# Attention results and turns of the fourth unit kind in pairs at every second token step, with separate tiles for the conditioning rows

## The chip, the cores and the metric

The kernel runs on one core of a Trainium2 chip. The metric is the device time of one execution in microseconds, the median of several. Before the change it is 1508.83 us (three runs, 1507.0 to 1510.0).

The names used below are those of the profile: PE is TensorE (matmuls; PEld is its loading of weights), DVE is VectorE, ACT is ScalarE, POOL is GpSimd, and SP is the engine whose queue issues most of the transfers.

## The reference

The kernel computes one layer of an encoder, on 1024 tokens of width 1024, in float32. Cut to what matters here:

```python
mod = silu(c) @ w_ada + b_ada                    # conditioning: six rows of 1024
h = rms_norm(x) * (1 + sc1) + sh1
proj = h @ w_in                                  # q, k, v of both mixers, and gates
o_a = neighbourhood_attention(norm(qa), norm(ka), va, rpb)      # 8 heads, 16 x 64 grid
o_g, lse_g = dilated_window_attention(rope(norm(qb)), rope(norm(kb)), vb, win, dil)  # 3 groups of 4 heads
o_b = sum over the 3 groups of softmax(lse)[g] * o_g
merged = sigmoid(gate_a) * (o_a @ w_proj_a) + sigmoid(gate_b) * (o_b @ w_proj_b)
x = x + gt1 * (merged @ w_o)
x = x + gt2 * (SwiGLU FFN of the normed, modulated x)
```

## The kernel before

**Stages.** A first stage normalises and turns x into `hT` and computes the first conditioning rows. Then comes the attention stage (some 58 to 614 us in the profile), which this change is about, then the rest of the gates, the merge with the output projection, and the feed-forward layer. A float32 operand of the large products is split into a high and a low part (`wsplit`, lines 114 to 120: ScalarE makes the high part, GpSimd or VectorE the low one), and three products of the parts are added (`PASS`).

**Units and token steps.** Attention works on ten units of two heads each. Units 0 and 1 are of kind 0, units 2 and 3 of kind 1, units 4 and 5 of kind 2 (the three dilations); units 6 to 9 are of kind 3, the fourth kind, which is the neighbourhood attention. The loop `for n in range(6, 92)` at line 922 goes through token steps: step n projects q, k and v of token tile t of unit u, where u, t = divmod(n, 8), in eight chunks of three matmuls of 128x384 (`proj_chunk`, L312). After the tenth unit, from step 80, the chunks are those of a part of the gates (`gate_pre`, L712, 128x512). After its eight chunks a step runs `proj_post`, which normalises q and k (the tiles `qn`) and sends v to DRAM (`v_d`).

**The middle of a step.** Between the fourth and the fifth chunk stand the small matmuls of attention, of units whose projection is done:

- scores of an item, that is of 128 queries of two heads against one to three blocks of 128 keys (`at_scores`, L476, in two PSUM banks of tag "s"; each is six matmuls, with 64 rows of the array for a head), followed by the softmax (`at_qk`: L490 on VectorE, L491 on ScalarE, L493 and L494 on VectorE), which leaves P;
- results of an item (`at_pv`, L517, in a bank of tag "v", with 64 columns of the array for a head), copied by ScalarE (L520) and stored (L521);
- turns (transposes) of q and k of token tiles (`qk_turns`, L377, in a bank of tag "v"), split into high and low parts by `qk_parts` (L399 and L400 on ScalarE, L401 and L402 on VectorE);
- turns of P of an item (`at_turn`, L502): one bank of tag "t" for each head, copied into PT by ScalarE for the first head (L508) and by VectorE for the second (L506).

Each of the tags "d", "s", "v" and "t" has two banks.

**Which step does what.** Items of kinds 0 to 2 go in clusters of up to four key blocks at every odd step (L543, L553, L555, L568, L575, L577, L588, L596 are their counterparts). From step 58 on (`PAIRED`), the items of kind 3 go one at every step: step n has the scores of one item (`cur`), the results of the item of two steps before (`done`), the turns of q and k of one token tile, that of step n - 2, and the turns of P of the item of one step before (`prev`), in this order. An item needs q and k of all eight token tiles of its unit.

**Other work of the stage.** The conditioning rows of the later stages, 4096 values, are made on VectorE: `ada_step` adds one of 64 tiles `wa` of 128x512, times a value of silu(c), to a sum (L299, L301) at seven of eight steps; two of them are loaded in one transfer of 512 KB (`ada_load`, L283). After eight, `ada_row` sums over partitions with a matmul into a bank of tag "t" (L271), VectorE adds the bias (L275), and the row is stored (L276). `t_piece` makes operands of the gate products from loads of `h_d` (tiles `tp`, L753 and on). `combine_step`, at steps 65 to 76, weighs the results of kinds 0 to 2 (L672 on TensorE in a bank of tag "t", L680 to L683 on VectorE). `bias_tabs` loads two bias tables for each unit of kind 3 (L424). The fetch of v from DRAM (L362 to L366) is issued at the end of the last token step of a unit.

**Tiles and order.** One pool tag, "big", has eight tiles of 4 KB a partition. It serves v, the bias tables, two rows' tiles `wa` at a time, `tp`, the combined results, gate results and more; a load into a tile can only go when an earlier user is done. TensorE's instructions stay in the order of the program in the whole kernel. Those of the other engines, and the transfers on SP's queue, are put in order by a planner that simulates the program; each engine then takes its instructions strictly in that order.

Of the kernel before, what the change touches and what calls it, by code (L numbers as in the profile page):

```python
# [36 lines left out]
PAIRED, RBT, COMB = 58, 5, 64  # L37
# [6 lines left out]
def hybrid_layer(ctx: ExitStack, tc: tile.TileContext, x, colp, wada1, wada2, bada2, wqkv, wg, wpa, wpb,  # L44
# [104 lines left out]
    NBIG, NLAND = 8, 7  # L149
# [6 lines left out]
    for tag, n, bufs in (("bm", 512, 1), ("p", 512, 4), ("qn", 256, 7), ("rtab", 512, 1), ("acc2", 512, 1), ("pT", 512, 4),  # L156
                         ("stg", 512, 3), ("vs", 128, 2), ("ra", 64, 2), ("rb", 64, 2)):
# [120 lines left out]
    def ada_load(i):  # L278

        if i < 64 and i not in ada_acc.setdefault("w", {}):  # L280
            c, kk = divmod(i, 8)
            ada_acc["w"][i] = big("wa2", [128, 2, 512])
            nc.sync.dma_start(ada_acc["w"][i], wada2[c, :, kk:kk + 2, :])  # L283

    def ada_step():
# [7 lines left out]
        if kk % 2 == 0:  # L293
            ada_load(i)
            ada_load(i + 2)
        wa = ada_acc["w"][i - kk % 2][:, kk % 2, :]
# [27 lines left out]
    def proj_post(U, t):  # L324
# [23 lines left out]
        else:  # L348
# [7 lines left out]
            if t == 7:  # L356
                U.v = big("v", [128, 8, 128])
# [7 lines left out]
            elif t == 7:  # L365
                nc.sync.dma_start(U.v, vd.rearrange("(p j) d -> p j d", j=8))  # L366
# [142 lines left out]

    @urgent(AV)  # L510
    def at_pv(I):
        U, nq, nkb = I.U, I.nq, I.nkb
        po = bank("v")
        for i in range(nkb):
            for h in range(2):
                hs = slice(h * 64, h * 64 + 64)
                nc.tensor.matmul(po[hs, :nq], U.v[:, I.kb0 + i, hs], I.PT[h][:, i, :nq],  # L517
                                 start=(i == 0), stop=(i == nkb - 1))
        st = ap_.tile([128, 128], F32, tag="stg", bufs=3, name="stg")
        nc.scalar.activation(st[:, :nq], po[:, :nq], AF.Copy)  # L520
        nc.scalar.dma_start(I.dst, st[:, :nq])  # L521
        if I.last:
            unit_out(U)
# [251 lines left out]
    ready = {}  # L775
# [143 lines left out]
    waiting = []  # L919
    raws = {}  # L920
    nextw = {}
    for n in range(6, 92):
# [16 lines left out]
        if t == 2 and 1 <= u <= 10:  # L939
            for slot, I in unit_items(units[u - 1]):  # L940
                if I.U.kind < 3:
                    waiting.append(I)
                else:
                    ready.setdefault(8 * u + 2 + slot, []).append(I)
# [5 lines left out]
        if n >= PAIRED:  # L950
            done, prev, cur = prev, cur, ready.pop(n, [])
        elif n % 2:
# [5 lines left out]
        else:  # L958
            done = []
# [9 lines left out]
        if PAIRED <= n <= 81 or 9 < n < PAIRED and n % 2:  # L969
            turns += [(units[m // 8], m % 8) for m in ((n - 2,) if n >= PAIRED else (n - 3, n - 2)) if m >= 8]  # L970
# [695 lines left out]
```

## Time and profile before

| | |
|---|---|
| median of the runs | 1508.83 us |
| the profiled execution | 1508.52 us, of which span 1506.7 us |
| busy: PE, PEld, DVE, ACT, POOL | 1485.7, 1265.1, 1090.2, 668.2, 535.1 us |
| granted TensorE clock | 0.999 |
| transfers | 241.65 MB, 160 GB/s on the mean |

The profile is one execution. A busy line gives the time of an engine's instructions, without issues of transfers, semaphores and branches. In the rows of the timeline the first number is the start in us from the begin of the span, the second the time until the end of the last instruction of the row; "xN" is the number of instructions in it, and what stands in brackets is the time for which the engine had been idle and who released it. Matmuls are pipelined, so that the end of one lies behind the start of the next; intervals are therefore read from start to start. In the groups by line, the numbers behind the count are busy us, mean ns of one, and the idle time just before them. In the rows of waits, they are us in total, times, and the longest.

### The profile page before, as it was taken

The page shows a single profiled execution, that of the slowest core. Times are in us where ns is not written, and L with a number is a line of the kernel's source. Part 1 is how long each engine was busy: PE and PEld are TensorE (multiplying, and loading weights), DVE is VectorE, ACT ScalarE, POOL GpSimd, SP SyncE. Part 2 cuts the span into 40 slices and gives each one's busy share as a digit, 9 for nine tenths or more (in the row PEclk, how much of TensorE's full clock was granted, in tenths as well). Part 3 has the DMA queues.
Part 4 walks back from the last instruction along what each step waited for, and adds up shares of the span by engine and source line. Part 5 has one row for each costly group of instructions (what it writes and reads, how often), then busy time and mean ns, then how long its engine had stood idle before and what let it go on. Part 6 is the DMA issues. An engine that isn't in the chain of part 4 may idle for free. (4 is left out here: it accounts for less than half of the span.)

```text
span 1506.7 us, 24201 instructions
## 1 busy us (share of the span) xinstructions
PE 1485.7 (99%) x8156; PEld 1265.1 (84%) x8156; DVE 1090.2 (72%) x2265; ACT 668.2 (44%) x1691; POOL 535.1 (36%) x540
## 2 busy tenths in 40 slices
PE   9999999999999999999999999999999999999998
PEld 7998989998888877788888888888888888887886
DVE  6867767767889845367675597788767777599468
ACT  5555655555645554246432354233223323354442
POOL 0432332321100040002352301676767776104464
PEclk9999999999999999999999999999999999999999
DMA  9625445645245164824553225345433334898342
GB/s 373 236 85 179 144 132 162 196 139 166 61 131 168 45 197 143 327 85 128 161 195 137 90 90 181 126 127 181 155 125 109 108 106 144 278 372 281 98 153 100
DMA packets 150637, 241.65 MB, mean 160 GB/s; under 512 B 26464, under 2 KB 69088, under 8 KB 149744
## 3 DMA queue, kind: packets, MB, share of 16 engines
q1 hardware_dynamic: 131936, 226.45, 45.7%
q10 hardware_dynamic: 18576, 13.64, 2.8%
q8 instruction: 65, 1.06, 0.3%
q14 instruction: 60, 0.49, 0.1%
HBM read 179.89 MB, written 60.15 MB: 159 GB/s over the span
## 5 line engine op out<-in xcount | busy, mean ns | idle before, releaser
L119 POOL TENSOR_TENSOR wlo<-raw,whi 128x512 fp32r<-128x512 f32 (+2 forms) x133 | 172.9, 1314 | 461.7 <-ACT whi L118 287.0
L118 ACT ACTIVATE whi<-raw 128x512 fp32r<-128x512 f32 (+1 forms) x348 | 203.6, 599 | 252.4 <-PE ps_s L1501 42.3
L312 PE MATMUL ps_d<-whi,hT 128*128 128x384 f32 x1152 | 310.8, 341 | 0.0
L119 DVE TENSOR_TENSOR wlo<-raw,whi 128x512 fp32r<-128x512 f32 (+1 forms) x215 | 183.6, 867 | 76.8 <-ACT whi L118 72.4
L312 PEld LDWEIGHTS ps_d<-whi,hT 128*128 128x128 f32 x1152 | 209.9, 188 | 5.2 <-ACT vs L350 3.5
L312 PE MATMUL ps_d<-wlo,hT 128*128 128x384 f32 x576 | 193.6, 336 | 2.9 <-DVE wlo L119 2.7
L312 PEld LDWEIGHTS ps_d<-wlo,hT 128*128 128x128 f32 x576 | 108.7, 189 | 4.0 <-DVE wlo L119 3.4
L118 ACT ACTIVATE whi<-ws 128x512 fp32r<-128x512 f32 x65 | 40.8, 628 | 126.9 <-DVE ws L1348 79.8
L1281 POOL TENSOR_TENSOR e<-e,c 128x512 f32<-128x512 f32 x44 | 68.9, 1565 | 59.2 <-DVE c L1411 35.0
L342 POOL TENSOR_TENSOR ra<-qn,rtab 128x64 f32<-128x64 f32 x48 | 16.3, 340 | 156.7 <-DVE qn L335 105.8
L119 POOL TENSOR_TENSOR wlo<-m,whi 128x512 fp32r<-128x512 f32 x35 | 51.4, 1479 | 54.5 <-ACT whi L118 54.5
L1279 ACT ACTIVATE e<-e 128x512 f32<-128x512 f32 x44 | 27.5, 631 | 95.1 <-DVE e L1414 66.4
L555 ACT ACTIVATE P<-P,st 128x256 f32<-128x256 f32 (+2 forms) x100 | 45.8, 460 | 41.4 <-DVE st L553 41.3
L712 PE MATMUL ps_d<-hT,whi 128*128 128x512 f32 x192 | 60.6, 397 | 0.0
L1331 PE MATMUL ps_v<-h2T,whi 128*128 128x512 f32 x192 | 59.2, 389 | 0.0
L1331 PE MATMUL ps_s<-h2T,whi 128*128 128x512 f32 x192 | 59.1, 389 | 0.0
L129 ACT ACTIVATE ry<-ss,eps 128x4 f32<-128x4 f32 (+1 forms) x88 | 26.2, 298 | 70.1 <-DVE ss L333 56.7
L1331 PE MATMUL ps_d<-h2T,whi 128*128 128x512 f32 x184 | 56.8, 390 | 0.0
L491 ACT ACTIVATE P<-P,sx 128x384 f32<-128x384 f32 (+1 forms) x64 | 37.1, 580 | 43.6 <-DVE sx L490 43.4
L119 DVE TENSOR_TENSOR wlo<-ws,whi 128x512 fp32r<-128x512 f32 x45 | 49.7, 1105 | 8.0 <-ACT whi L118 7.8
L1280 DVE TENSOR_TENSOR e<-e 128x512 f32<-128x512 f32 x44 | 42.5, 973 | 17.8 <-ACT e L1279 17.7
L301 DVE SCALAR_TENSOR_TENSOR acc<-wa,cact,acc 128x512 f32<-128x512 f32 x56 | 42.6, 762 | 16.8 <-DMA wa<-in_wada_dram 16.5
(445 smaller groups left out, 3956.8 us busy)
## 6 DMA issues: line engine op xcount, KB each, us to landing
raw<-in_w_dram SPq DMA_DIRECT2D x139, 256.0 KB
ga_d<-e SPq DMA_DIRECT2D x77, 256.0 KB
raw<-ga_d SPq DMA_DIRECT2D x77, 256.0 KB
wa<-in_wada_dram SPq DMA_DIRECT2D x32, 512.0 KB
raw<-in_wqkv_dram SPq DMA_DIRECT2D x80, 192.0 KB
m<-in_w_dram SPq DMA_DIRECT2D x44, 256.0 KB
raw<-in_wg_dram SPq DMA_DIRECT2D x42, 256.0 KB
xt<-in_x_dram SPq DMA_DIRECT2D x16, 512.0 KB
```

What stands on the lines that cost most here:

```text
L118: nc.scalar.activation(hi[:, :n], r, AF.Copy)
L119: (eng or nc.gpsimd).tensor_sub(lo[:, :n], r, fview(hi[:, :n]))
L129: nc.scalar.activation(y, ss, AF.Ln, scale=1.0 / n, bias=eps)
L301: nc.vector.scalar_tensor_tensor(ada_acc[c], wa, cact[:, kk:kk + 1], ada_acc[c], op0=ALU.mult, op1=ALU.add)
L312: nc.tensor.matmul(pd[:, :384], tok(a, k, t), U.w[k][b][:, :384], start=(k == 0 and i == 0), stop=(k == KT - 1 and i == 2))
L491: nc.scalar.activation(P[:nq, :nk], P[:nq, :nk], AF.Exp, scale=-1.0, bias=nm, accum_out=sm)
L555: nc.scalar.activation(C.P[h][:nq, c], C.P[h][:nq, c], AF.Exp, scale=-1.0, bias=nm, accum_out=sm)
L712: nc.tensor.matmul(st["p"], gw[i, br][j][a][:, kk * 128:(kk + 1) * 128], hT[b][:, k, hs], start=(k == 0 and q == 0), stop=(k == 7 and q == 2))
L1279: nc.scalar.activation(sg, a, AF.Sigmoid)
L1280: nc.vector.tensor_mul(sg, sg, a)
L1281: nc.gpsimd.tensor_mul(sg, sg, up)
L1331: nc.tensor.matmul(pb, w[p][:, k * 128:(k + 1) * 128], b[q][:, k], start=(k == 0 and i == 0), stop=(k == 3 and i == 2))
```

## The change

- Items of kind 3 go in pairs. At an odd step the middle has, in this order: the results of both items of the pair of four steps before (`pair_pv`, in one bank, with one copy and one store), the turns of P of the first item of the pair of two steps before, the turns of q and k of two token tiles (as for the other kinds), the turns of P of the second item, and the scores of the first item of the new pair. The middle of an even step has the scores of the second item alone. The first pair is taken at step 59, where the first item was at step 58; a step 92, which has no chunks, gives the last results.
- The conditioning rows have two tiles of their own (tag "wa", 2 KB a partition each) and come in 64 loads of 256 KB, one step ahead; "big" has seven tiles.
- v of kind 3 gets its tile and is fetched three steps later (`v_back`, at the token step at which the unit's items are listed).

The kinds 0 to 2 keep their clusters and their order. The diff, cut to its core:

```diff
-PAIRED, RBT, COMB = 58, 5, 64
+RBT, COMB = 5, 64
-    NBIG, NLAND = 8, 7
+    NBIG, NLAND = 7, 7
-                         ("stg", 512, 3), ("vs", 128, 2), ("ra", 64, 2), ("rb", 64, 2)):
+                         ("stg", 512, 3), ("wa", 512, 2), ("vs", 128, 2), ("ra", 64, 2), ("rb", 64, 2)):
...
-            ada_acc["w"][i] = big("wa2", [128, 2, 512])
-            nc.sync.dma_start(ada_acc["w"][i], wada2[c, :, kk:kk + 2, :])
+            ada_acc["w"][i] = ap_.tile([128, 512], F32, tag="wa", bufs=2, name="wa2")
+            nc.sync.dma_start(ada_acc["w"][i], wada2[c, :, kk, :])
...
-        if kk % 2 == 0:
-            ada_load(i)
-            ada_load(i + 2)
-        wa = ada_acc["w"][i - kk % 2][:, kk % 2, :]
+        ada_load(i)
+        ada_load(i + 1)
+        wa = ada_acc["w"][i]
...
-            if t == 7:
+            if t == 7 and U.kind < 3:
                 U.v = big("v", [128, 8, 128])
...
-            elif t == 7:
-                nc.sync.dma_start(U.v, vd.rearrange("(p j) d -> p j d", j=8))
...
+    def v_back(U):
+        U.v = big("v", [128, 8, 128])
+        nc.sync.dma_start(U.v, v_d[U.u - 2].rearrange("(p j) d -> p j d", j=8))
+
     @urgent(AV)
-    def at_pv(I):
-        U, nq, nkb = I.U, I.nq, I.nkb
+    def pair_pv(pair):
+
         po = bank("v")
-        for i in range(nkb):
-            for h in range(2):
-                hs = slice(h * 64, h * 64 + 64)
-                nc.tensor.matmul(po[hs, :nq], U.v[:, I.kb0 + i, hs], I.PT[h][:, i, :nq],
-                                 start=(i == 0), stop=(i == nkb - 1))
-        st = ap_.tile([128, 128], F32, tag="stg", bufs=3, name="stg")
-        nc.scalar.activation(st[:, :nq], po[:, :nq], AF.Copy)
-        nc.scalar.dma_start(I.dst, st[:, :nq])
-        if I.last:
-            unit_out(U)
+        for j, I in enumerate(pair):
+            for i in range(I.nkb):
+                for h in range(2):
+                    hs = slice(h * 64, h * 64 + 64)
+                    nc.tensor.matmul(po[hs, j * 128:(j + 1) * 128], I.U.v[:, I.kb0 + i, hs], I.PT[h][:, i, :],
+                                     start=(i == 0), stop=(i == I.nkb - 1))
+        st = ap_.tile([128, 256], F32, tag="stg", bufs=3, name="stg")
+        nc.scalar.activation(st, po[:, :256], AF.Copy)
+        nc.scalar.dma_start(pair[0].o[:, pair[0].q0:pair[0].q0 + 256], st)
...
-    for n in range(6, 92):
+    for n in range(6, 93):
...
-                if I.U.kind < 3:
-                    waiting.append(I)
-                else:
-                    ready.setdefault(8 * u + 2 + slot, []).append(I)
+                (waiting if I.U.kind < 3 else pairs).append(I)
+            if units[u - 1].kind == 3:
+                v_back(units[u - 1])
...
-        if n >= PAIRED:
-            done, prev, cur = prev, cur, ready.pop(n, [])
-        elif n % 2:
+        if n % 2 or n == 92:
             done, prev, cur = prev, cur, []
             if waiting:
                 cur = [Cluster()]
                 while waiting and cur[0].keys + waiting[0].nkb * 128 <= 512:
                     cur[0].add(waiting.pop(0))
-        else:
-            done = []
+            elif pairs:
+                cur = [pairs.pop(0), pairs.pop(0)]
...
-        if PAIRED <= n <= 81 or 9 < n < PAIRED and n % 2:
-            turns += [(units[m // 8], m % 8) for m in ((n - 2,) if n >= PAIRED else (n - 3, n - 2)) if m >= 8]
+        if 9 < n <= 81 and n % 2:
+            turns += [(units[m // 8], m % 8) for m in (n - 3, n - 2) if m >= 8]
...
-        if n >= PAIRED or n % 2 or n < 10:
-            for I in cur:
-                if I.__class__ is Cluster:
-                    cl_scores(I)
-                    cl_qk(I)
-                else:
-                    at_scores(I)
-                    at_qk(I, 0)
-                    at_qk(I, 1)
-            for I in done:
-                (cl_pv if I.__class__ is Cluster else at_pv)(I)
+        def pair_scores(I):
+            at_scores(I)
+            at_qk(I, 0)
+            at_qk(I, 1)
+
+        if n % 2 or n < 10 or n == 92:
+            if len(cur) == 1:
+                cl_scores(cur[0])
+                cl_qk(cur[0])
+            if done:
+                cl_pv(done[0]) if len(done) == 1 else pair_pv(done)
+            if len(prev) == 2:
+                at_turn(prev[0], 0)
+                at_turn(prev[0], 1)
             for j in range(0, len(turns), 2):
                 qk_turns(turns[j:j + 2], "s" if n < 10 else "v")
-            for I in prev:
-                if I.__class__ is Cluster:
-                    cl_turn(I)
-                else:
-                    at_turn(I, 0)
-                    at_turn(I, 1)
+            if len(prev) == 2:
+                at_turn(prev[1], 0)
+                at_turn(prev[1], 1)
+            elif prev:
+                cl_turn(prev[0])
+            if len(cur) == 2:
+                pair_scores(cur[0])
+        elif len(cur) == 2:
+            pair_scores(cur[1])
```

More of the change, by code (lines that the diff above doesn't have):

```diff
@@ L774, in hybrid_layer @@
     units = []
-    ready = {}
     extra = {}
@@ L918, in hybrid_layer @@
     cur, prev, done = [], [], []
-    waiting = []
+    waiting, pairs = [], []
     raws = {}
     nextw = {}
-    for n in range(6, 92):
+    for n in range(6, 93):
         u, t = divmod(n, 8)
```

## The prediction

> **What bounds the kernel now.** I read the page first, then the busy time by stage, then who TensorE and VectorE waited for in the attention stage, then single token steps in the timeline.
>
> ```profile
> span 1506.7 us, 24201 instructions
> PE 1485.7 (99%) x8156; PEld 1265.1 (84%) x8156; DVE 1090.2 (72%) x2265; ACT 668.2 (44%) x1691; POOL 535.1 (36%) x540
> ```
> TensorE works for 1485.7 of 1506.7 us. Its instructions run in the order of the program, so time is gained only where its instructions come closer together or where a wait of it goes. The change is confined to the attention stage, from 58 to 614 us.
>
> ```profile
> 58.00:614.00 556.00, 545.69 (x3793) 485.82 (x3793) 403.29 (x1309) 307.85 (x1048) 128.16 (x251) 1.00 0.45 140
> 245.00:365.00 120.00, 119.89 (x892) 112.38 (x891) 85.24 (x298) 73.25 (x260) 32.55 (x64) 1.00 0.48 151
> 422.00:522.00 100.00, 98.24 (x718) 86.24 (x717) 90.04 (x294) 53.19 (x189) 6.22 (x5) 1.00 0.37 113
> ```
> The columns are stretch, length, then busy time of PE, PEld, DVE, ACT and POOL, the granted clock, the DMA share and GB/s. In the whole stage TensorE is idle for 556.00 - 545.69 = 10.3 us; that is about all that a better order can win. Where VectorE is busy for 85.24 of 120 us (71%) TensorE loses 0.1 us; where it is busy for 90.04 of 100, 1.8 us. So late VectorE work is the suspect, and the waits say so:
>
> ```profile
> PE ps_d L312 <- DVE wlo L119: 2.7, 1, 2.7
> PE ps_t L672 <- DVE PT L506: 1.4, 2, 1.0
> PE ps_v L377 <- DVE rz L132: 1.2, 1, 1.2
> DVE acc L301 <- DMA wa<-in_wada_dram: 16.5, 8, 4.4
> ```
> The columns are us in total, times, longest. VectorE takes its instructions in order, and eight times it stood for a tile of conditioning rows (`wa`), 16.5 us in all. Three of its waits for a DMA lie just ahead of these three waits of TensorE:
>
> ```profile
> 140.89 0.75 DVE L301 SCALAR_TENSOR_TENSOR acc<-wa,cact,acc 128x512 f32<-128x512 f32 x1 [1.53 <-DMA wa<-in_wada_dram]
> 210.70 1.46 DVE L753 TENSOR_TENSOR tp<-tp 128x512 f32<-128x512 f32 x1 [2.05 <-DMA tp<-h_d]
> 418.31 0.75 DVE L301 SCALAR_TENSOR_TENSOR acc<-wa,cact,acc 128x512 f32<-128x512 f32 x1 [3.41 <-DMA wa<-in_wada_dram]
> ```
> Both `wa` and `tp` live in the eight "big" tiles, which they share with `v`, the bias tables and the gate results, so a load goes out only when one of these is free. The stall behind the second row cost more than its wait:
>
> ```profile
> 215.70 0.45 PE L312 MATMUL ps_d<-wlo,hT 128*128 128x384 f32 x1 [2.67 <-DVE wlo L119]
> 215.70:219.60 3.90, 3.90 (x14) 3.50 (x14) 2.64 (x12) 1.72 (x7) 1.23 (x5) 0.63 0.28 85
> ```
> After 2.67 us without work the granted clock was 0.63 for 3.9 us. Its 14 matmuls at the 0.17 us of the step below would take 2.4, so 1.5 us more were lost: 4.2 in all.
>
> **The change part by part.** The sum is made against the profiled execution, 1508.52 us (span 1506.7 and 1.8 around it, which stays); the median of the runs, 1508.83, is 0.3 higher.
>
> *The order on TensorE.* One ordinary step of the fourth kind, from the last matmul of the first half of the projection:
>
> ```profile
> 451.20 0.34 PE L312 MATMUL ps_d<-whi,hT 128*128 128x384 f32 x1
> 451.46 0.79 PE L476 MATMUL ps_s<-qk 64*128 64x384 f32 x6
> 452.19 0.88 PE L517 MATMUL ps_v<-PT,v 128*64 128x128 f32 x12
> 452.99 0.44 PE L377 MATMUL ps_v<-ident,qn 128*128 128x128 f32 x2
> 453.27 0.82 PE L502 MATMUL ps_t<-ident,P 128*128 128x128 f32 x6
> 453.84 0.42 PE L312 MATMUL ps_d<-whi,hT 128*128 128x384 f32 x1
> 454.10 0.33 PE L312 MATMUL ps_d<-wlo,hT 128*128 128x384 f32 x1
> 454.27 0.34 PE L312 MATMUL ps_d<-whi,hT 128*128 128x384 f32 x1
> ```
> Starts tell more than durations, since matmuls overlap. A projection matmul follows another after 0.17 us (454.10 to 454.27). The way into the scores takes 0.26, so 0.09 is lost when the array goes from 128x128 to 64 rows. From 451.20 to 454.10 are 2.90 us; two steps cost 5.80. No matmul is saved by pairing; the question is what the new order costs in such changes of shape. Those that this step lacks, projection to results and results to projection, stand at the end of the stage, with 512 columns:
>
> ```profile
> 610.23 0.39 PE L712 MATMUL ps_d<-hT,wlo 128*128 128x512 f32 x1
> 610.55 0.66 PE L517 MATMUL ps_v<-PT,v 128*64 128x128 f32 x8
> 611.14 0.74 PE L712 MATMUL ps_d<-hT,whi 128*128 128x512 f32 x2
> 611.72 0.40 PE L712 MATMUL ps_d<-hT,wlo 128*128 128x512 f32 x1
> 611.95 0.40 PE L712 MATMUL ps_d<-hT,whi 128*128 128x512 f32 x1
> ```
> An ordinary interval here is 0.23 (611.72 to 611.95); the way into the results takes 0.32, again 0.09 more, and the two matmuls after them take 0.58 in place of 0.46, so coming back costs 0.12 in the first interval. Eight matmuls of results take 0.59 with their exit and twelve 0.80, so one is 0.053. Worked out of this, an odd step after the change is: into the results 0.26; two items' results 0.80 + 12 x 0.053 = 1.44; sixteen transposes (six, four of q and k, six) at 0.11, with 0.06 for the first (q and k take 0.28 in place of 0.22) 1.82; into the scores 0.09 more than a transpose, as from the projection; scores with their exit 0.73; the first projection interval 0.17 + 0.12 = 0.29: 4.63. An even step is 0.26 + 0.73 + 0.29 = 1.28. Together 5.91, against 5.80: 0.11 a pair slower, with 16 pairs **+1.8 us**. Transposes to scores and scores to projection are not in the trace; if each of the three is off by 0.1, the pair is 0.2 cheaper to 0.4 dearer, -3 to +6. I take +1.8, from the nearest rows.
> The Trainium skill, "TensorEngine Tiling (Array Packing)", Key Properties, says that changing the tiling mode drains TensorE. The 0.26 against 0.17 agrees. A count by that rule alone has six changes in two steps before (into scores, results and turns of each) and six after, so this term would be 0 and not +1.8.
>
> *The work that goes from VectorE and ScalarE.* Each pair of tiles of q and k is now split by four instructions in place of eight.
>
> ```profile
> L401 DVE SCALAR_TENSOR_TENSOR qk<-ps_v,hg,qk 128x128 fp32r<-128x128 f32 x24 | 10.7, 444 | 0.2 <-ACT qk L400 0.2
> L402 DVE TENSOR_TENSOR qk<-ps_v,qk 128x128 fp32r<-128x128 f32 x24 | 9.3, 386 | 0.0
> L401 DVE SCALAR_TENSOR_TENSOR qk<-ps_v,hg,qk 128x256 fp32r<-128x256 f32 x23 | 11.7, 507 | 7.0 <-ACT qk L400 6.9
> L402 DVE TENSOR_TENSOR qk<-ps_v,qk 128x256 fp32r<-128x256 f32 x23 | 10.1, 441 | 0.0
> L506 DVE COPY PT<-ps_t 128x384 f32<-128x384 f32 x24 | 13.1, 546 | 0.0
> L508 ACT ACTIVATE PT<-ps_t 128x384 f32<-128x384 f32 x24 | 11.9, 498 | 0.0
> ```
> The last number ahead of the second bar is the mean in ns. VectorE gives up 24 x 0.83 - 12 x 0.95 = 8.5 us; of it seven pairs, 5 us, between 422 and 522, where 90% becomes 85%. ScalarE's half of the split shrinks likewise, and 16 copies and stores of results go. None of this is on TensorE, so by itself it is worth nothing; it is worth what it does to the stalls below.
>
> *The first item of the kind.* In the step that begins at 367 us TensorE stands for the parts of q and k:
>
> ```profile
> 369.02 0.50 PE L476 MATMUL ps_s<-qk 64*128 64x256 f32 x4 [0.95 <-DVE qk L402]
> ```
> After the change these scores come at the end of the next step's middle, later by a step, whose 24 projection matmuls alone take 24 x 0.17 = 4.1 us, and nothing else is late there: **-0.9**, 0 to -0.95.
>
> *The copies of the turned P.* The new wait: both items' turns need four banks of tag "t", and there are two. The second item's first turn starts six transposes of the first and four of q and k after that, 0.06 + 10 x 0.11 = 1.16 us after the first item's. The third transpose starts at 0.28 and takes about 0.27 itself (0.82 for six, the last begun at 0.55), so it is done at 0.55; ScalarE's copy of 0.50 ends at 1.05 if it starts at once. That just fits: 0 to 0.1 us a pair. If it starts late, TensorE stands, and behind it the turn, the scores and the second half of the projection. The nearest row is the wait for such a copy with 1.4 us in two times, 0.7 each, 11 us for 16 pairs. I take 0.1, **+1.6**, since at that place the scores' VectorE work of the same step, which now competes with the copy, has moved behind the turns; both ends stay for the range.
>
> *The conditioning rows and `v`.* The rows come as 64 loads of half the size into two tiles of their own, one step ahead; seven big tiles remain for the others.
>
> ```profile
> L283 SPq DMA_DIRECT2D wa<-in_wada_dram x32: 327/423/799, 54.6 to 477.2; - x32
> SPq L366 <- DMA v_d<-vs: 20.5, 2, 19.9
> ```
> 32 more issues at 0.42 us are 13.5 us of SP's queue over 420 us; behind them stand the weight loads, which have steps to spare. The fetch of `v` goes to the queue three steps later, past the loads of these steps, and by then its stores are long done, for which it now holds the queue (once for 19.9 us); none of TensorE's waits names a load behind it. `v` is first needed five steps after the new place. For both: nothing on the path. But `tp`, bias and `v` no longer wait for a big tile behind rows, and the rows not for one of those. The three stalls shown, 5.3 us of wait and 1.5 of clock, hang on such loads: I count 80%, 5.4, as gone. The other 10.3 - 0.9 - 5.3 = 4.1 us of idle time hang on a full VectorE: with 85% for 90%, 30%, 1.2. Together **-6.6**, from 0 to -10.9.
>
> **The sum**: +1.8 - 0.9 + 1.6 - 6.6 = -4.1: 1504.4 for the profiled execution, **1504.7** for the median.
>
> **The rivals.**
> *The second item waits for its banks (slower).* ScalarE or VectorE is in the middle of other work when the turns are done, every pair. At 0.7 us each: +11.2 + 1.8 - 0.9, and with VectorE as late as this supposes only half of the 6.6: +8.8, 1517.6. It decides from (6.6 + 0.9 - 1.8) / 16 = 0.36 us a pair. For it: VectorE's 90%. Against: TensorE's standing gives VectorE time to catch up. The Trainium skill, "TensorEngine Tiling (Array Packing)", PSUM Bottleneck, warns of this: tiling speeds up TensorE but not the evacuation of PSUM, whose copy may become the bottleneck.
> *The loads stay late (no change).* With two tiles a load can go only when VectorE is done with the row two before, so a late VectorE delays SP's queue, and that VectorE again; only the 1.2 is won: +1.8 - 0.9 + 1.6 - 1.2 = +1.3, 1510.1. For it: eight waits in 32 loads with room for more rows ahead; against: they came in bursts, when a big tile came free. The Trainium skill, "DMA: Bandwidth & Descriptors", Rules for kernel authors, asks for 1 MiB a transfer, which speaks against halving them; no row here has the same rows in halves.
> *All stalls go.* +1.8 - 0.9 - 10.9 and no new wait: -10, 1498.8.
>
> **How the numbers follow.** About 0.2%, 3 us, is what a measurement of this kernel can tell from no change. The forecast has 0.40 (0.33 faster, 0.06 same, 0.01 slower, by its unsure terms), all stalls gone 0.10 (faster), the late loads 0.28 (0.02, 0.19, 0.07), the banks 0.22 (0.01, 0.02, 0.19). That gives faster 0.46, same 0.27, slower 0.27. The range goes from the stalls' case, half of it left out, 1497, to short of the full price of the banks, 1514.
>
> **What would show it.** In the profile after: rows L401 and L402 with 12 of 128x256 at 0.5 and 0.44 us; odd middles of 4.6 us and even ones of 1.3 between the projection's halves; no wait at the kind's first scores; `wa` waits of VectorE well under 16.5 us and no clock of 0.63 near 215 us. Wrong it is if TensorE waits for PT's copies (L506, L508) at the second turn of many odd steps, or if its idle time in the stage stays near 10 us.

## The result, and the profile after

The change makes the kernel slower: 1530.85 us median (1529.07 to 1536.91, four runs) against 1508.2 us (1507.0 to 1510.0, four runs beside them), a ratio of 1.0156, 95% interval 1.0126 to 1.0187. The forecast was 1504.7 with a range up to 1514. The profiled execution after took 1536.91 us, 28.4 more than the one before. It is the longest of its four runs, 6.1 us above their median, so the lengths that are read from it below add up to more than the 22.7 us between the medians.

The page of the kernel after, span and TensorE:

```profile
span 1535.1 us, 24166 instructions
PE 1498.8 (98%) x8156; PEld 1273.4 (83%) x8156; DVE 1089.0 (71%) x2241; ACT 670.2 (44%) x1651; POOL 540.5 (35%) x540
```

The instructions of TensorE are as many as before, but they take 13.1 us longer (1485.7 before), and the rest of the 28.4 us is idle time. Where did it arise? Each token step has 24 projection matmuls from step 6 on, so the first of any step can be counted out in the timeline. In each of the next two fences, before and then after, the first row is the first matmul of step 6 and the second the first gate product behind the attention:

```profile
58.68 0.33 PE L312 MATMUL ps_t<-whi,hT 128*128 128x384 f32 x1
614.03 0.61 PE L731 MATMUL ps_v<-hT,whi 128*128 128x512 f32 x2
```
```profile
64.63 0.33 PE L311 MATMUL ps_t<-whi,hT 128*128 128x384 f32 x1
644.44 0.73 PE L731 MATMUL ps_v<-hT,whi 128*128 128x512 f32 x2
```

Step 58, where the fourth kind begins, starts at 365.5 before and at 377.0 after. So there are three losses: 5.9 us in the start, 5.5 in steps 6 to 58, and 19.0 in the paired stage (248.5 to 267.5 us). The first lies outside the stage to which the prediction confined the change. Behind the gates 2 us come back.

**The paired stage.** Stretches of after (length, busy time of PE, PEld, DVE, ACT and POOL, granted clock), and the like stretch of before:

```profile
377.00:644.00 267.00, 253.10 (x1633) 210.97 (x1633) 175.50 (x538) 126.78 (x362) 29.39 (x24) 0.97 0.39 122
422.00:522.00 100.00, 92.90 (x645) 81.22 (x646) 80.10 (x257) 48.37 (x153) 5.80 (x5) 0.95 0.37 110
```
```profile
366.00:614.00 248.00, 243.25 (x1637) 204.31 (x1636) 177.83 (x566) 124.59 (x401) 30.09 (x24) 1.00 0.43 133
```

TensorE's idle time grows from 4.75 to 13.9 us, and its matmuls take 9.85 us longer, at a clock of 0.97 where it was 1.00. Who ends the idle time is told by the waits of TensorE from 365 to 660 us (us in total, times, longest):

```profile
PE ps_t L499 <- ACT PT L505: 7.1, 9, 2.5
PE ps_t L499 <- DVE PT L503: 5.3, 5, 2.0
PE ps_d L311 <- DVE wlo L119: 2.9, 1, 2.9
PE ps_v L374 <- DVE qn L334: 1.1, 1, 1.1
PE ps_t L499 <- DVE row L275: 0.3, 1, 0.3
```

The two first rows are the copies of the turned P, 12.4 us in 14 waits: the very rows by which the prediction said it would be wrong. Two of these waits in the timeline of after:

```profile
505.26 0.63 ACT L118 ACTIVATE whi<-raw 128x512 fp32r<-128x512 f32 x1 [2.32 <-DMA raw<-in_wg_dram]
506.58 0.48 ACT L505 ACTIVATE PT<-ps_t 128x384 f32<-128x384 f32 x1
507.11 1.12 PE L499 MATMUL ps_t<-ident,P 128*128 128x128 f32 x4 [2.52 <-ACT PT L505]
...
621.20 0.69 DVE L767 TENSOR_TENSOR w1m<-w1m 128x512 f32<-128x512 f32 x1 [2.69 <-DMA w1m<-in_w_dram]
621.81 0.55 DVE L503 COPY PT<-ps_t 128x384 f32<-128x384 f32 x1
622.41 0.31 PEld L499 LDWEIGHTS ps_t<-ident,P 128*128 128x128 f32 x3 [2.24 <-DVE PT L503]
622.41 0.55 PE L499 MATMUL ps_t<-ident,P 128*128 128x128 f32 x3 [2.00 <-DVE PT L503]
```

In both the bank is full in time and the copy takes 0.5 us; but the copying engine stands, in its fixed order, at an instruction of quite other work (a gate weight, a mix of weights), whose load has not landed. Four of the 14 waits, 7.2 of the 12.4 us, lie like this right behind a late load (at 490, 507, 555 and 622 us). Five of 0.3 us each are in the odd steps from 83 on, which have no q and k to turn between the two items, so that the copy's own time shows. The other five, 3.7 us, lie behind other work of the copying engine. Before the change a bank came to the turns of P again only a step later, and none of these turns waited for a copy; only the other users of these banks did (L672 and L271, 2.0 us in four waits from 58 to 614 us). The longest stall then costs once more, in clock:

```profile
507.00:520.00 13.00, 12.89 (x64) 11.71 (x65) 8.55 (x28) 5.86 (x20) 1.46 (x2) 0.74 0.05 17
```

A clock of 0.74 for 13 us is a loss of 3.4 us, more than the wait of 2.52 itself.

**The start.** SP's queue in the start of after: the loads of rows (`wa`) go out among those that the start needs.

```profile
20.05 0.33 SPq L178 DMA_DIRECT2D land<-in_wada_dram  x1
21.28 0.81 SPq L283 DMA_DIRECT2D wa<-in_wada_dram  x2
23.05 0.33 SPq L178 DMA_DIRECT2D land<-in_wada_dram  x1
...
34.83 0.33 SPq L283 DMA_DIRECT2D wa<-in_wada_dram  x1
37.30 0.33 SPq L178 DMA_DIRECT2D land<-in_wada_dram  x1
38.77 0.33 SPq L283 DMA_DIRECT2D wa<-in_wada_dram  x1
```

And what TensorE does then, with the clock of the stretch behind it:

```profile
29.85 0.64 PE L788 MATMUL ps_t<-land,c 128*32 128x256 f32 x8 [1.62 <-DMA land<-in_wada_dram]
40.73 0.61 PE L803 MATMUL ps_t<-ones,rowk 128*128 128x1 f32 x4 [1.71 <-ACT rowk L794]
```
```profile
41.00:46.00 5.00, 5.00 (x32) 4.40 (x33) 4.68 (x10) 3.07 (x7) 0.00 (x0) 0.67 1.03 399
```

Before, the first load of rows left at 54.57 us and neither wait was there:

```profile
54.57 1.10 SPq L283 DMA_DIRECT2D wa<-in_wada_dram  x2
```

The two waits and the clock of 0.67 over 5 us make 5.0 of the 5.9 us. Before, the big tiles were full until the start had used its landing tiles (seven of the eight; the other has `v` of the first unit). That shortage had kept the rows out; nothing in the program's order does.

**Steps 6 to 58.** VectorE's waits for the rows, 16.5 us in eight times before, did not shrink (after, 64 to 644 us):

```profile
DVE acc L300 <- DMA wa<-in_wada_dram: 18.0, 18, 2.6
```

The stalls behind the loads near 141, 211 and 418 us are gone, as predicted (of the first, a wait of 1.30 us, 0.62 is left), and others have come in their stead. Counted in the same way, steps 6 to 34 take 4.9 us less than before, and steps 34 to 58 take 10.4 us more, with waits of TensorE of 1.36, 1.32 and 2.93 us at 294, 313 and 369 us.

### The profile page after: what moved, and what is told of

It is laid out like the page before. It is cut to its first block, busy times and chain, and to the rows that moved or that the text cites. A ratio compares the mean times of both kernels' runs of the same rounds, so it can differ in the third digit from the quotient of the medians.

```text
span 1535.1 us, 24166 instructions
## 1 busy us (share of the span) xinstructions
PE 1498.8 (98%) x8156; PEld 1273.4 (83%) x8156; DVE 1089.0 (71%) x2241; ACT 670.2 (44%) x1651; POOL 540.5 (35%) x540
## 3 DMA queue, kind: packets, MB, share of 16 engines
q10 hardware_dynamic: 16272, 13.64, 2.7%
## 4 chain that ended last, share of the span: by engine, by line
PE 81%; DMA 8%; DVE 6%; ACT 2%; issue 2%; POOL 1%; SPq 0%; ACTq 0%; DVEq 0%; POOLq 0%
PE ps_d L311 13%; PE ps_v L1333 7%; PE ps_d L1333 7%; PE ps_s L1333 7%; PE ps_t L1333 6%; PE ps_d L712 4%; DMA wa<-in_wada_dram 4%; PE ps_s L1503 3%; PE ps_v L1503 3%; PE ps_d L1503 3%; PE ps_t L1503 3%; PE ps_d L1268 2%; PE ps_s L1268 2%; PE ps_v L731 2%; PE ps_s L731 2%
## 5 line engine op out<-in xcount | busy, mean ns | idle before, releaser
L119 POOL TENSOR_TENSOR wlo<-raw,whi 128x512 fp32r<-128x512 f32 (+2 forms) x133 | 176.4, 1339 | 480.5 <-ACT whi L118 342.4
L311 PEld LDWEIGHTS ps_d<-whi,hT 128*128 128x128 f32 x1152 | 212.0, 190 | 11.8 <-ACT vs L349 5.7
L1283 POOL TENSOR_TENSOR e<-e,c 128x512 f32<-128x512 f32 x44 | 68.9, 1565 | 58.9 <-DVE c L1413 34.7
L1333 PE MATMUL ps_v<-h2T,whi 128*128 128x512 f32 x192 | 59.2, 389 | 0.0
```

The costliest lines, as they stand in the source:

```text
L119: (eng or nc.gpsimd).tensor_sub(lo[:, :n], r, fview(hi[:, :n]))
L311: nc.tensor.matmul(pd[:, :384], tok(a, k, t), U.w[k][b][:, :384], start=(k == 0 and i == 0), stop=(k == KT - 1 and i == 2))
L1283: nc.gpsimd.tensor_mul(sg, sg, up)
L1333: nc.tensor.matmul(pb, w[p][:, k * 128:(k + 1) * 128], b[q][:, k], start=(k == 0 and i == 0), stop=(k == 3 and i == 2))
```

## The experiments

Theory after reading the traces: two separate causes. The second use of the two banks within one middle exposes TensorE to every late copy (paired stage); and the rows' two small tiles let loads out too early in the start and hold them up later. Rivals: the rows' loads alone made all engines late, the copies too; or the new order costs on TensorE itself.

In the table are the medians, ratios to the kernel before on the same chip with their 95% intervals, and the lengths counted from the profiled execution: start (to step 6), steps 6 to 58, step 58 to the gates. These lengths come from a single execution each: the last row is the same kernel as "four tiles, held", and its steps 6 to 58 took 305.6 us in place of 313.4. A difference of some us in such a length shows little by itself; the ratios with their intervals count for more.

| kernel | median us | ratio | start | 6 to 58 | 58 to gates |
|---|---|---|---|---|---|
| before | 1508.2 | 1 | 58.7 | 306.8 | 248.5 |
| after | 1530.85 | 1.0156 (1.0126-1.0187) | 64.6 | 312.3 | 267.5 |
| rows' two tiles alone | 1517.88 | 1.0078 (1.0052-1.0104) | 63.9 | 312.0 | 247.9 |
| pairs alone | 1518.93 | 1.0076 (1.0050-1.0102) | 59.5 | 305.4 | 264.1 |
| after, turns split | 1521.94 | 1.0094 (1.0061-1.0127) | 65.6 | 314.1 | 249.6 |
| after, tiles held in the start | 1526.13 | 1.0121 (1.0096-1.0146) | 59.3 | 312.4 | 260.5 |
| pairs alone, turns split | 1511.78 | 1.0021 (1.0004-1.0038) | 59.4 | 306.4 | 253.3 |
| pairs alone, no cover | 1522.84 | 1.0100 (1.0058-1.0142) | 59.2 | 302.5 | 266.1 |
| q and k in pairs alone | 1506.91 | 0.9992 (0.9977-1.0007) | 58.9 | 304.9 | 249.2 |
| two tiles, GpSimd's queue | 1529.96 | 1.0141 (1.0108-1.0173) | 64.0 | 319.7 | 252.1 |
| seven big tiles alone | 1507.80 | 1.0003 (0.9985-1.0020) | 59.3 | 302.2 | 246.9 |
| single loads alone | 1511.16 | 1.0028 (1.0014-1.0042) | 59.6 | 305.0 | 254.7 |
| four tiles | 1513.18 | 1.0052 (1.0032-1.0073) | 64.9 | 307.0 | 247.1 |
| four tiles, held | 1508.93 | 1.0009 (0.9994-1.0024) | 59.2 | 313.4 | 247.0 |
| two tiles, held | 1516.37 | 1.0052 (1.0037-1.0066) | 58.9 | 311.4 | 248.4 |
| four tiles, held, again | 1506.36 | 0.9999 (0.9986-1.0013) | 59.0 | 305.6 | 247.3 |

**The two halves apart.** First the kernel before with the memory half of the diff alone; then the kernel after with the rows as before. The core of the second edit, against the kernel after:

```
-    NBIG, NLAND = 7, 7
+    NBIG, NLAND = 8, 7
...
-            ada_acc["w"][i] = ap_.tile([128, 512], F32, tag="wa", bufs=2, name="wa2")
+            ada_acc["w"][i] = big("wa2", [128, 2, 512])
...
```

> The kernel before with only the change's memory half: two tiles of their own for the conditioning rows (loads of half the size, one step ahead), seven big tiles, the fourth kind's `v` fetched three steps later. Items stay single. My theory (two separate causes): the start loses 6 us and steps 6 to 58 lose 5.5, as in the profile after, and the paired stage loses nothing: about +11, 1517 to 1522; first proj_chunk near 64.6 us in place of 58.7. Rival, the rows alone made VectorE and ScalarE late everywhere: +20 to +28, 1528 to 1536, with the stage from 367 us on 15 us or more longer. The prediction on record had this half at -6.6, 1502.

> The kernel after with the conditioning rows as before (eight big tiles, loads of two rows): the order in pairs alone, with `v` three steps later. My theory: first proj_chunk back at 58.7 us, steps 6 to 58 as before, and the paired stage (step 58 to the gates) still 13 to 19 us longer than before's 246.6, since the second item's turns stand for copies of the turned P: 1520 to 1528. Rival, the rows' loads alone made the copies late: no wait for these copies over 0.3 us and 1506 to 1511. Rival, the new order costs in itself on TensorE (changes of shape): the stage longer by as much, but spread evenly over the 16 pairs and without waits.

The tiles alone cost 11.8 us (0.78% of 1508), in the start and in steps 6 to 58; the pairs alone 11.5 us (0.76%; 1518.93 us is a little under the 1520 to 1528 expected), in the paired stage. Together 1.54%, where the whole change costs 1.56%: two causes, which add up. The first rival falls: with the rows as before, the waits for the copies are still there (pairs alone, 365 to 630 us):

```profile
PE ps_t L500 <- ACT PT L506: 4.2, 7, 1.8
PE ps_t L500 <- DVE PT L504: 3.6, 4, 1.5
```

The third reading, that the new order costs as much by its changes of shape, falls with a pair of that kernel that has no such wait of note. It lasts from the scores of one odd step to those of the next; beside it stands one step of before:

```profile
510.02 0.79 PE L474 MATMUL ps_s<-qk 64*128 64x384 f32 x6
...
523.44 0.79 PE L474 MATMUL ps_s<-qk 64*128 64x384 f32 x6
```
```profile
511.33 0.79 PE L476 MATMUL ps_s<-qk 64*128 64x384 f32 x6
...
518.07 0.79 PE L476 MATMUL ps_s<-qk 64*128 64x384 f32 x6
```

The pair takes 13.42 us with 20 matmuls of results, so 13.64 with 24 (at 0.055), less 0.05 of a short wait inside the second item's turns; two steps of before take 13.48. That is 0.11 us for this pair, just what the prediction summed.

**The second use of the banks taken away.** The second item is turned in the even step (only the last pair's, at step 91, stays):

```
             if len(prev) == 2:
                 at_turn(prev[0], 0)
                 at_turn(prev[0], 1)
...
-            if len(prev) == 2:
+            if len(prev) == 2 and n == 91:
                 at_turn(prev[1], 0)
                 at_turn(prev[1], 1)
...
-        elif len(cur) == 2:
-            pair_scores(cur[1])
+        else:
+            if len(prev) == 2:
+                at_turn(prev[1], 0)
+                at_turn(prev[1], 1)
+            if len(cur) == 2:
+                pair_scores(cur[1])
```

> The kernel after with the second item's turns moved from the odd step to the even step behind it, ahead of that step's scores: results, q and k still go in pairs, but a bank of the turned P is used again only a step later. My theory: the waits for its copies (12.4 us in 14 times) and the clock lost behind them go, for 0.1 us a pair more in changes of shape: 14 to 17 us less than after, 1514 to 1518, the paired stage near 250 us. Rival, VectorE and ScalarE are late because of loads and TensorE would stand for something else of theirs: within 4 us of after, 1527 to 1531, with other waits in the same places.

> The order in pairs with the conditioning rows as before, and the second item's turns in the even step, a step behind the first's, so that no bank of the turned P is used twice in a middle. My theory (the reuse of the two banks is the whole cost of the pairs): the 12 us of the pairs alone go, no wait for a copy of the turned P over 0.5 us is left, the stretch from step 58 to the gates is 248 to 251 us (before 248.5), in all 1505 to 1510, within 0.2% of before or about it. Rival, the new order costs in changes of shape on TensorE, evenly over 16 pairs: 4 to 8 us over before with no waits to show for it.

In the first kernel the paired stage came to 249.6 us as expected, from 267.5. The total missed by 4 us: its start and steps 6 to 58 were 2.8 us longer than after's, and the saving had been reckoned from an execution of after that was 6.1 us above the median. In the second, the pairs' cost of 11.5 us became 3.2 (0.21%), and the intervals of the two (1.0050 to 1.0102, 1.0004 to 1.0038) lie apart. So the second use of the banks within one middle is most of the pairs' price, 8.3 us. The rest is not: 1511.78 us and 253.3 in the paired stage are above the 1505 to 1510 and 248 to 251 expected. There are fewer waits for the copies, but one of 3.4 us in step 74, so "none over 0.5" was wrong, too (pairs alone, turns split, 365 to 620 us). ScalarE had then stood 3.70 us for VectorE, and VectorE 1.98 for a late row.

```profile
PE ps_t L500 <- ACT PT L506: 3.7, 2, 3.4
```

**Less cover.** With the rows as before, q and k are turned behind both items' turns instead of between them:

```
                 at_turn(prev[0], 0)
                 at_turn(prev[0], 1)
+                at_turn(prev[1], 0)
+                at_turn(prev[1], 1)
             for j in range(0, len(turns), 2):
...
```

> The order in pairs with the rows as before (1518.9), but q and k are turned behind both items' turns, so that nothing of TensorE lies between the two uses of the banks where a step has turns of q and k (steps 61 to 81, 11 pairs). The prediction on record had 1.16 us from the first item's turns to the second's against a copy ready at 1.05; here 0.72 is left. If the copies come when the banks are full (their own time sets it): 0.3 to 0.5 us more a pair, 4 to 6 us, 1523 to 1525. Rival, the copies are late only where ScalarE or VectorE stands behind a load, and then by far more than 0.44: within 2 us of 1518.9.

It went towards the first reading, but by less: 1522.84 us is just short of its range, the intervals of the two totals overlap, and it is the trace that shows the difference. There are 20 waits in place of 11, and 11.6 us in place of 7.8; eight of the eleven pairs without cover wait 0.25 to 0.27 us, where 0.3 to 0.5 was expected.

```profile
PE ps_t L500 <- ACT PT L506: 7.7, 16, 1.9
PE ps_t L500 <- DVE PT L504: 3.9, 4, 1.6
```

Both kinds of wait exist: short ones where the copy's own time doesn't fit, and long ones, up to 1.9 us here, where its engine comes to it late.

**One part alone, for VectorE.** Kernel before, q and k two tiles at a time:

```
-        if PAIRED <= n <= 81 or 9 < n < PAIRED and n % 2:
-            turns += [(units[m // 8], m % 8) for m in ((n - 2,) if n >= PAIRED else (n - 3, n - 2)) if m >= 8]
+        if 9 < n <= 81 and n % 2:
+            turns += [(units[m // 8], m % 8) for m in (n - 3, n - 2) if m >= 8]
```

> The kernel before with one part of the change alone: the fourth kind's q and k are turned two tiles at a time at every second step; results, scores and turns of P stay one item a step, rows as before. It takes 8.5 us from VectorE and some from ScalarE. My theory (their work is worth nothing where TensorE does not stand for it, and the stalls hang on loads): 1505 to 1509, no difference. Rival, the idle 4.1 us behind a full VectorE shrink and the first item's 0.95 goes: 2 to 4 us less, 1503 to 1505.

No difference that can be measured (the interval leaves room for 3.5 us less and 1.1 more). The work taken from VectorE is worth that little by itself, and there is less of it than was said (below).

**The start.** The start's own small matrix of activations is put into the rows' two tiles (it had a tile of its own), so they come free only when the start is over:

```
-    c32 = ap_.tile([128, 256], F32, tag="sq", bufs=1, name="c32").rearrange("p (k n) -> p k n", k=8)
+    c32 = []
+    for i in range(2):
+        c32.append(ap_.tile([128, 512], F32, tag="wa", bufs=2, name="c32")[:, :128].rearrange("p (k n) -> p k n", k=4))
...
```

> The kernel after with the two tiles of the conditioning rows held during the start by the start's own small matrix of activations (two tiles in place of its own one), so that no load of rows can go out among the loads of the start. My theory: the 6 us of the start are these loads' place in SP's queue: first proj_chunk back at 58.7 and 5 to 6 us less than after, 1525 to 1526. Rival, the start of the profiled run after was only disturbed: the start is as long, or the total is within 1.5 us of after (1530.85).

The first projection of step 6 is back at 59.3 us, the total 0.35% lower in ratio, 5.3 us. The intervals of the two totals overlap, but other rows of the table say the same. The start ends at 63.9 to 65.6 us in all five kernels whose rows have tiles of their own that are free from the beginning, and at 58.7 to 59.6 in the other eleven rows. With four tiles, the same hold takes the total from 1.0052 (1.0032 to 1.0073) to 1.0009 and 0.9999, whose intervals lie below that. Steps 6 to 58 stay long.

**Steps 6 to 58.** In the kernel with the tiles alone SP stood 53.2 us between 60 and 375 us with a load of rows at the head of its queue (all rows of that line among its waits, summed), 6.5 us before. Is it the queue, the missing big tile, the half-size loads, or that two tiles are too few? One kernel issues the rows on GpSimd's queue, one has seven big tiles and nothing else, one loads the rows singly out of the eight big tiles, and one has four own tiles, loads three steps ahead, and six big ones:

```
-            nc.sync.dma_start(ada_acc["w"][i], wada2[c, :, kk, :])
+            nc.gpsimd.dma_start(ada_acc["w"][i], wada2[c, :, kk, :])
```
```
-    NBIG, NLAND = 8, 7
+    NBIG, NLAND = 7, 7
```
```
-            ada_acc["w"][i] = big("wa2", [128, 2, 512])
+            ada_acc["w"][i] = big("wa2", [128, 512])
...
```
```
-    NBIG, NLAND = 7, 7
+    NBIG, NLAND = 6, 6
...
-            ada_acc["w"][i] = ap_.tile([128, 512], F32, tag="wa", bufs=2, name="wa2")
+            ada_acc["w"][i] = ap_.tile([128, 512], F32, tag="wa", bufs=4, name="wa2")
...
+        ada_load(i + 2)
+        ada_load(i + 3)
```

> The rows in their own two tiles with single items (1517.9), the 64 loads of rows issued on GpSimd's queue in place of SP's. In the profile of the tiles alone SP stood 53 us between 60 and 375 us with a load of rows at its head (before 6.5), and weight and `tp` loads behind it. My theory: that hold is the 5.2 us of steps 6 to 58, so they come back to about 307 us (tiles alone 312.0, before 306.8), unless GpSimd's own work now stands behind the loads. Rival, VectorE's own waits for rows (14.6 us in 15 times) are the cause: 311 to 313 as before. In the start, the loads still go out among those of the start: first proj_chunk 61 to 64.

> The kernel before with one edit: seven big tiles in place of eight; rows as before, in pairs, out of the big tiles; single items. It tells whether the big tile that is gone costs the 5 us that steps 6 to 58 lost with the rows' own tiles (312.0 against 306.8). If the tile is the cause: 310 to 313 in that stretch, 1511 to 1514. If the rows' two small tiles are (loads at the head of the queue, waiting for VectorE): 305 to 308, 1505 to 1509.

> The kernel before with the rows loaded one at a time (64 loads of half the size, one step ahead, as in the change), but out of the eight big tiles as before; single items. If the size and number of the loads cost the 5 us of steps 6 to 58: 310 to 313 there. If the two tiles of their own do, since a load must wait in the queue for the row two before: 305 to 308, and SP's standing with a row at its head stays under 20 us between 60 and 375 us (before 6.5, own tiles 53).

> The rows' own tiles with single items (1517.9), but four of them, three steps ahead, and six big tiles (six landing tiles in the start, which changes it: only steps 6 to 58 are compared). If a load's wait for the row two before is the cause, four tiles take most of it away: 306 to 309 in steps 6 to 58 and under 30 us of SP with a row at its head. If the lost big tiles are the cause, it gets worse than 312: 313 to 320.

The queue as such is not it: on GpSimd's the loads stand as well, and the total of 1.0141 is worse than the 1.0078 of SP's queue, so that expectation of mine failed. The missing big tile costs nothing that can be measured (1.0003). Single loads show no loss in this stretch either (305.0; SP's wait with a row at its head: 12.5 us), but 0.28%, 4 us, in all, and the paired stage has 254.7 for 248.5. There the trace names two waits behind late rows:

```profile
365.22 0.75 DVE L300 SCALAR_TENSOR_TENSOR acc<-wa,cact,acc 128x512 f32<-128x512 f32 x1 [2.77 <-DMA wa<-in_wada_dram]
369.94 0.80 PE L475 MATMUL ps_s<-qk 64*128 64x256 f32 x4 [2.81 <-DVE qk L401]
```

This wait was 0.95 us before; another, of 2.50 us at 424 (before 0.98), follows a row that came 1.93 us late, and behind each the clock was 0.87 over 13 us, 1.7 us each. Four tiles bring the stretch back to 307.0, with 19.7 us of SP. But this start differs, and a first kernel with four tiles and an undisturbed start read 313.4, in a profiled execution 6 us above the median of its own runs:

```
+    for i in range(4):
+        c32.append(ap_.tile([128, 512], F32, tag="wa", bufs=4, name="c32")[:, :64].rearrange("p (k n) -> p k n", k=2))
...
```

> Four own tiles for the rows and six big ones, single items (1513.2), with all four tiles held in the start by the start's own small matrix of activations, so that the rows can go out only behind it. My theory (the start's 6 us are the rows' loads among its own): first proj_chunk near 59 us (64.9 with the four tiles alone), steps 6 to 58 near 307, in all 1505 to 1509: the rows' cost gone whole, and no measurable gain over before, since TensorE was idle for 10 us only. Rival, six landing tiles delay the start by themselves: first proj_chunk 62 to 65 and 1511 to 1514. If it beats before, it does so by 0.1 to 0.2%.

So two and four tiles, both held in the start, were run beside each other on one chip:

> Single items, two own tiles for the rows (seven big ones, `v` three steps later), both held in the start by its own small matrix, so that the start is as before and only steps 6 to 58 can differ. If two tiles are too shallow (a load waits in SP's queue for the row two before): 5 to 7 us over before by the medians, 1.003 to 1.005, while the same with four tiles lies at 1.001. If the four tiles' gain was chance: both alike, within 0.1% of each other.

> The kernel with four own tiles, held in the start, six big ones and single items, once more, on one chip with the one above: its profiled execution was 6 us over the median of its runs. If depth is what counts: 1.000 to 1.002, and a load of rows at the head of SP's queue stands for under half of what it does with two tiles. If not: within 0.1% of the kernel with two.

1.0052 (1.0037 to 1.0066) with two, 0.9999 (0.9986 to 1.0013) with four: the depth is the cause, that is, the tiles and how far ahead they are loaded together, 0.53% or 8 us. (The two kernels also differ by a big tile, which the one with four lacks.) VectorE's waits for rows between 60 and 375 us, two tiles, then four:

```profile
DVE acc L302 <- DMA wa<-in_wada_dram: 10.8, 14, 1.6
```
```profile
DVE acc L304 <- DMA wa<-in_wada_dram: 4.6, 6, 2.4
```

SP's standing with a row at its head fell from 64.2 to 39.0 us, less than I had expected. The late loads are made rarer, not impossible: the execution with 313.4 had waits of 1.74 and 2.61 us at 291 and 365, as the kernels with two tiles have. With four tiles the rows cost nothing that can be measured, and they gain nothing either: no version here beats the kernel before by more than can be measured.

## Why the prediction was wrong

*The order on TensorE* (+1.8): right, 0.11 us in the one pair that can be read without a wait.

*VectorE's relief* (8.5 us, worth nothing by itself): its worth was right, its size not. The rows of after, 377 to 644 us:

```profile
L398 DVE SCALAR_TENSOR_TENSOR qk<-ps_v,hg,qk 128x256 fp32r<-128x256 f32 x12 | 8.1, 674 | 2.9 <-ACT qk L397 2.7
L399 DVE TENSOR_TENSOR qk<-ps_v,qk 128x256 fp32r<-128x256 f32 x13 | 8.0, 616 | 0.0
```

A pair of the fourth kind takes 0.674 + 0.616 = 1.29 us, not 0.95: the price was the mean of a group that holds mostly the other kinds, whose code writes the tile in another pattern (that the pattern is the reason was not tried). The profile before had the right price in the same groups, read from 366 to 614 us alone:

```profile
L401 DVE SCALAR_TENSOR_TENSOR qk<-ps_v,hg,qk 128x256 fp32r<-128x256 f32 x1 | 0.7, 675 | 0.0
L402 DVE TENSOR_TENSOR qk<-ps_v,qk 128x256 fp32r<-128x256 f32 x1 | 0.6, 565 | 0.0
```

The relief is 24 x 0.83 - 12 x 1.29 = 4.4 us.

*The first item's wait* (-0.9): right; nothing of it is left among the waits after.

*The copies of the turned P* (+1.6): this step failed. It held 1.16 us of cover against 1.05 us of copy and took 0.1 us a pair, "since at that place the scores' VectorE work [...] has moved behind the turns". It asked what else this middle puts on the two engines, and not what may stand at their head: work on gate weights, weight mixes and rows, whose loads come late now and then. It also gave the cover of q and k to all 16 pairs, where the last five have none (steps 83 to 91; 0.31 us each in after). Measured: the pairs alone cost 11.5 us, order and all, and 8.3 of it, 0.5 a pair, went when the second use of the banks was taken out of the middle. The rival of the banks, with a chance of 0.22, named the mechanism, but took every pair to lose 0.7. In the pairs alone it was 11 waits of 0.3 to 1.8 us and lost clock (0.74 over 13 us from 398 us on), so it is partly luck that its 11.2 us for these waits comes so near.

The Trainium skill, "TensorEngine Tiling (Array Packing)", PSUM Bottleneck, had been cited for this rival: the copy out of PSUM may become the bottleneck. The trace agrees in that such copies stopped TensorE. But they did not get slower (128x384 on ScalarE 498 ns before and 499 after, on VectorE 546 and 552); most of the time was lost because they began late.

*The conditioning rows* (-6.6): this step failed too, by sign: +11.8. "Nothing on the path" for 32 more loads looked at the steps where rows were loaded before, and "the change is confined to the attention stage" left out the start, where the full big tiles alone had kept the rows away. And the rival of the late loads (two tiles let a load go only when VectorE is done with the row two before) had the mechanism, but no price beyond the lost gain; by the runs of two and four tiles it costs 8 us. That the three named stalls would go was right (4.9 us up to step 34); the same late loads then stopped other steps. One row of them was misread: the wait of 1.2 us for `rz` stood at 86 us, and the one behind the row at 141 is 1.3 us for GpSimd's `qn`, which hardly changes the sum.

What stays open: which late load ends each wait is read from the traces, not tried, for the copies and for the single loads out of the big tiles alike; and what the last 3.2 us of the pairs with split turns are made of, beyond the order's 1.8 and the one long wait.

## What to carry to other kernels

When a change lets a resource be used twice within one stretch, the time of the copy between the uses is the least that must be hidden: look at what stands ahead of it on its engine, and above all whether that can wait for a load, because the engine's order is fixed. A buffer of its own takes a load out of a shortage, but it also takes away what kept that load late: ask where it will be issued now, and give it the depth that it had (four halves here, not two).

## What the runs showed of the hardware

A wait of TensorE sometimes costs clock behind it, and its length alone does not tell when. After a single wait of 2.52 us the granted clock was 0.74 over 13 us (3.4 us lost); after waits of 1.10, 0.45 and 0.32 us close together it was 0.87 from 427 to 440 (1.7 us lost); after a single wait of 1.35 us at 473 us it stayed at 1.00. These are rows of after:

```profile
427.00:440.00 13.00, 12.68 (x71) 11.68 (x71) 9.55 (x35) 5.99 (x21) 0.00 (x0) 0.87 0.34 117
473.00:483.00 10.00, 9.90 (x57) 7.90 (x57) 9.23 (x34) 5.55 (x18) 1.02 (x1) 1.00 0.34 110
```

But the stall that cost 1.5 us of clock at 216 us in the kernel before came again in the pairs alone, as long (2.68 us at 217), and left the clock at 1.00, while a single wait of 1.52 us in the kernel with q and k in pairs alone was followed by 0.87:

```profile
217.00:230.00 13.00, 13.00 (x95) 12.45 (x96) 8.51 (x32) 7.97 (x28) 3.12 (x12) 1.00 0.42 130
146.00:159.00 13.00, 12.99 (x84) 12.14 (x86) 8.71 (x31) 7.67 (x28) 4.14 (x10) 0.87 0.50 166
```

In the 16 profiled executions, from 45 to 1350 us, no wait that came to less than 1.5 us, alone or together with others within 4 us, was followed by a lower clock; from 1.5 to 2.9 us some were and some were not. Each of the 29 drops was a stretch of 3.4 us, or twice that, at a clock of 0.5. What decides between them, these runs do not show.
